# Gates interleaved with the first output row's product, and a first chunk loaded through ScalarE's queue, in a one-core RWKV-7 layer

## The chip, the cores and the metric

The kernel runs on one core of a Trainium2 chip. The metric is device time in microseconds (us), the median of several executions; less is better. The program is one launch that computes three blocks of a language model for one sequence of 1024 tokens of width 1024, in float32.

## The reference, cut to what matters

The model is a Hawk block (a gated linear recurrence), a feed-forward network (FFN) with a gated per-layer embedding (PLE), then an RWKV-7 block with its own FFN and PLE, and a block with a state-space branch and attention. The change is in the RWKV-7 block. Its core, per head of 64 channels, is a recurrence over the tokens:

```python
def step(S, inp):
    r_t, w_t, k_t, v_t, a_t, b_t = inp
    sa = jnp.einsum('bhvk,bhk->bhv', S, a_t)
    S = S * w_t[:, :, None, :] + sa[..., None] * b_t[:, :, None, :] + v_t[..., None] * k_t[:, :, None, :]
    y = jnp.einsum('bhvk,bhk->bhv', S, r_t)
    return S, y
...
yn = ((y - mean) * lax.rsqrt(var + RW_GN_EPS)).reshape(B, T, D)
yn = yn * ln_w.astype(f32) + ln_b.astype(f32)
...
g = jax.nn.sigmoid(xg @ g1) @ g2
out = (yn + bonus.reshape(B, T, D)).astype(x.dtype) * g
return out @ w_o, v_first
```

The output of the recurrence is normed per head, multiplied by a gate `g` (a product with the matrix g2, 160 rows), and multiplied by `w_o` (1024 by 1024); the result is added to the residual stream `h`.

## The kernel before, in words

**Layout and order.** The sequence is cut into two halves of 512 tokens. Activations stand as eight tiles of 128 channels by 512 tokens. The kernel is written as Python generators (FFN, PLE, recurrence, ...), and a helper `both` interleaves two of them by weights, so that TensorE has dense matmuls from the one beside the many small steps of the other. Every engine (TensorE, VectorE, ScalarE, GpSimd, SyncE) runs its own instruction list strictly in order. That order is fixed when the program is built: a planner goes through the program with costs of its own, and each engine takes of the instructions that are ready by the planner's reckoning the one that stands first in the program.

**Matmuls in float32.** Each product of a weight matrix with an activation is made of three faster ones, on a high part and a low part of each operand (`mm3`, L188 to L198: hi by hi at L196, hi by low at L197, low by hi at L198). A high part is a cast on ScalarE (L61 for weights, L201 for activations), a low part a subtraction on VectorE (L64 and L66 for weights, L202 for activations). With 8 blocks of 128 channels an output row of 128 channels by 512 tokens takes 24 matmuls.

**Weights.** `Weights` streams all matrices in one fixed order through two raw buffers, loaded on SyncE's queue (L52), and three pairs of split buffers. `get(key)` returns the next matrix and first makes sure that it and the one behind it have been split.

**The recurrence, `rw_b`.** It is called once per half, interleaved with FFN work. A half has 8 chunks of 64 tokens. `load(c)` loads a chunk's operands from DRAM, where earlier steps left them: the tile AR (L1030), KB in three loads (L1034 and twice L1038) and ST in two (L1043), all on SyncE's queue. `load_cp` loads for a pair of chunks the triangular tables TT (L1054) and T1 (L1055, T in the profile), twice each, and V (L1057). The first products of a half are those of AR with the state (L1138), then AR by KB (L1094), then those of T and TT (L1068). The tables are written to DRAM by the step before, in stores that SyncE issues as VectorE finishes them (L1009 for ttD, L1011 for t1D); the last of these stand right ahead of `load(0)` on SyncE's queue. The norm's weight `lnw` is one 4 KB piece a partition, the first tile of the recurrence's pool; it is loaded on GpSimd's queue (L1020) and read at the end of a pair of chunks (L1221). Tiles are placed in memory in the order in which they are allocated, and a new tile waits for the last use of the tiles whose memory it takes.

**The gate and the output, `rw_c`.** It is called once per half behind the recurrence. Eight gate steps come first: four matmuls with the two pieces of g2 (L1285), one VectorE operation that adds the bias to the normed output `qt` and multiplies it by the gate (L1286), and the split into high and low part. The `qt` tiles are loaded on GpSimd's queue, two at a time in half 1 and all four in half 0. Then come eight output rows m: the row's matrix ("ro", half, m), a load of `h`, `mm3` over the eight gated operands, the addition to `h` (L272), and the squares for the next norm. In half 0 six gate steps run alone, then a deferred norm of the other half, then the rest interleaved with `rw_shift(1)`, which is mostly VectorE work. In half 0 PSUM has the pools "mm" (3 banks), "g" (3) and two single ones; in half 1 "mm" (6) and "aux" (2).

Of the kernel before, what the change touches and what calls it, by code (L numbers as in the profile page):

```python
# [9 lines left out]
F32 = mybir.dt.float32  # L10
# [7 lines left out]
D = 1024  # L18
# [11 lines left out]
class Weights:  # L30
# [44 lines left out]
    def view(t, kp, nk, m):  # L75
        return t[0:kp, 0:nk * m].rearrange("p (k m) -> p k m", m=m)

    def get(self, key):
        i = self.pos
        assert self.jobs[i][0] == key, (self.jobs[i][0], key)  # L80
        n = len(self.jobs)
        while len(self.loaded) < min(n, i + self.nraw):
            if len(self.loaded) >= self.nraw + len(self.ready):
                self._split(len(self.ready))
            else:
                self._load(len(self.loaded))
        while len(self.ready) < min(n, i + 2):
            self._split(len(self.ready))
            if len(self.loaded) < n:
                self._load(len(self.loaded))  # L90
        self.pos += 1
        r = self.ready[i]
        self.ready[i] = None
        return r


class Kernel:
# [763 lines left out]
    def rw_elem(self, half, ap):  # L861
# [7 lines left out]
        def at(tag, bufs=2, dt=F32, n=HALF):  # L869
            return self.t512(tag, bufs, dt, n, ap)  # L870
# [25 lines left out]

        def products(j, AR, KB, rk):
            pb = self.psum("g")
# [7 lines left out]
            for ch in range(8):  # L906
                cp, par = ch // 2, ch % 2
                o = 64 if par == 0 else 0
                for e in range(2):
                    rows = slice(e * 64, e * 64 + 64)  # L910
                    nc.tensor.matmul(pe[e][o:o + 64, cp * 64:cp * 64 + 64], KB[rows, cp, 1 + par, :],
                                     AR[rows, cp, 1 + par, :], start=True, stop=True)
            for e in range(2):
# [11 lines left out]
        for j in range(8):  # L925
# [12 lines left out]
            s, c, kk = at("t_s", 1), at("t_c", 1), at("t_k", 1)  # L938
            AR = ap.tile([128, 4, 4, 64], F32, tag="AR", name="AR", bufs=2)
            KB = ap.tile([128, 4, 4, 64], F32, tag="KB", name="KB", bufs=2)  # L940
            R, K = AR[:, :, 0:4:3, :], KB[:, :, 0:4:3, :]
            A, B = AR[:, :, 1:3, :], KB[:, :, 1:3, :]
            B3 = B.rearrange("p a b c -> p a (b c)")
# [20 lines left out]
            gtt(out=R, in0=R, in1=v4(rr), op=MUL)  # L964
            nc.sync.dma_start(out=self.arD[half][j], in_=AR.rearrange("p a b c -> p (a b c)"))
            nc.sync.dma_start(out=self.kbD[half][j], in_=KB.rearrange("p a b c -> p (a b c)"))
# [47 lines left out]
    def rw_b(self, half, bp):  # L1014

        nc = self.nc
        tt = nc.vector.tensor_tensor
        mm = nc.tensor.matmul
        self.lnw = bp.tile([128, D], F32, name="lnw")
        nc.gpsimd.dma_start(out=self.lnw, in_=self.i["rw_ln_w"].to_broadcast([128, D]))  # L1020
        st = {}

        def odd(t, e, a=0, n=16):

            return t.rearrange("p (h v) -> p h v", v=64)[:, a + e:a + n:2, :]

        def load(c):
            s = st.setdefault(c, {})
            AR = bp.tile([128, 8, 128], F32, tag="AR", name="AR", bufs=2)
            nc.sync.dma_start(out=AR, in_=self.arD[half][:, :, c * 128:(c + 1) * 128].rearrange("j p x -> p j x"))  # L1030
            KB, src = bp.tile([128, 8, 128], F32, tag="KB", name="KB", bufs=2), self.kbD[half]

            r = self.hp(c % 2)
            nc.sync.dma_start(out=KB[r], in_=src[:, r, c * 128:(c + 1) * 128].rearrange("j p x -> p j x"))  # L1034
            r = self.hp(1 - c % 2)
            for a in range(2):
                o = c * 128 + (1 - a) * 64
                nc.sync.dma_start(out=KB[r, :, a * 64:(a + 1) * 64], in_=src[:, r, o:o + 64].rearrange("j p x -> p j x"))  # L1038
            s.update(AR=AR, KB=KB)

            s["ST"] = bp.tile([128, D], F32, tag="ST", name="ST", bufs=2)
            for e in range(2):
                nc.sync.dma_start(out=s["ST"][self.hp(e), :], in_=self.vD[half * 4 + c // 2, self.hp(c % 2), :])  # L1043

        def load_cp(cp):
            s = st.setdefault(("cp", cp), {})

            TT = bp.tile([128, 16, 64], F32, tag="TT", name="TT", bufs=2)
            T1 = bp.tile([128, 16, 32], F32, tag="T1", name="T1", bufs=1)
            for sd in range(2):  # L1050
                r = sd * 64
                of = lambda t: t.rearrange("x (h e a c) t -> x h e a (c t)", e=2, a=4, c=2)[:, :, 1 - sd, cp, :]
                to = lambda t: t.rearrange("x (h c) t -> x h (c t)", c=2)
                nc.sync.dma_start(out=to(TT[r:r + 64]), in_=of(self.ttD))  # L1054
                nc.sync.dma_start(out=to(T1[r:r + 32]), in_=of(self.t1D[half]))  # L1055
            V = bp.tile([128, D], F32, tag="V", name="V", bufs=2)
            nc.sync.dma_start(out=V, in_=self.vD[half * 4 + cp])  # L1057
            s.update(V=V, TT=TT, T1=T1)
# [42 lines left out]
        def kbt(c):  # L1101
# [3 lines left out]
            for g in range(2):  # L1105
# [3 lines left out]
                nc.scalar.copy(out=s["KT"][:, g * 512:(g + 1) * 512], in_=p)  # L1109

        load(0)
        load_cp(0)
        load(1)
        gram(0)
        merge(0)
# [3 lines left out]
        for c in range(8):  # L1119
# [5 lines left out]
            G, AR, KT, ST = s["G"], s["AR"], s["KT"], s["ST"]  # L1125
# [6 lines left out]
            for g in range(2):  # L1132

                for j in range(4 * g, 4 * g + 4):
                    for a in range(2):
                        for e in range(2):
                            r, o = self.hp(e), self.hp((a + e + c) % 2)
                            mm(zy[e][o, hs(j)], AR[r, j, a * 64:(a + 1) * 64], self.S[r, j, :], start=j == 0,  # L1138
                               stop=False, skip_group_check=True)
                for h in range(8 * g, 8 * g + 8):  # L1140
                    e = h % 2
                    mm(zy[e][ru[e], hs(h // 2)], G[rv[e], h, ga:ga + 64], ST[rv[e], hs(h)],
                       start=False, stop=False, skip_group_check=True)

                for e in range(2):
                    (nc.scalar.copy if e == 0 else nc.vector.tensor_copy)(
                        out=odd(Z, e, 8 * g, 8), in_=zy[e][:, g * 256:(g + 1) * 256].rearrange("p (h v) -> p h v", v=64))
            yield
            pp = self.psum2()
            for g in range(2):  # L1150
                p = pp[:, g, :]
# [3 lines left out]
                for e in range(2):  # L1155
                    (nc.scalar.copy if e == 0 else nc.vector.tensor_copy)(out=odd(ST[ru[e], :], e, 8 * g, 8),
                                                                          in_=odd(p[ru[e], :], e, 0, 8))
            pp = self.psum2()
            yield
            for g in range(2):  # L1160
                ps = pp[:, g, :]
                for h in range(8 * g, 8 * g + 8):
                    r = slice((h % 2) * 64, (h % 2) * 64 + 64)
# [16 lines left out]
            for g in range(2):  # L1180
                for h in range(8 * g, 8 * g + 8):
                    e = h % 2
                    mm(zy[e][rv[e], hs(h // 2)], G[:, h, gr:gr + 64], ST[:, hs(h)],
                       start=False, stop=True, skip_group_check=True)
                for e in range(2):
                    nc.scalar.copy(out=odd(Y[self.hp(c % 2), :], e, 8 * g, 8),
                                   in_=zy[e][rv[e], g * 256:(g + 1) * 256].rearrange("p (h v) -> p h v", v=64))
# [3 lines left out]
            if c < 6:  # L1191
                load(c + 2)
# [76 lines left out]
    def rw_c(self, half, op, nout, qs):  # L1269

        nc = self.nc
        tt = nc.vector.tensor_tensor
        hs = slice(half * HALF, (half + 1) * HALF)
        sh, sl, s3 = self.sg
        w = [self.W.get(("rg2", half, 0)), self.W.get(("rg2", half, 1))]
        o = {}
        for j in range(8):
            if j % 2 == 0 and len(self.qt) <= j // 2:
                next(qs)
            qt = self.qt[j // 2][:, j % 2, :]  # L1280
            p = self.psum()
            (wh, wl), (w3, _) = (tuple(t[:, 0, j * 128:(j + 1) * 128] for t in a) for a in w)
            pairs = ((wh, sh), (wh, sl), (wl, sh), (w3[0:96], s3[0:96, :]))
            for n, (a, x) in enumerate(pairs):
                nc.tensor.matmul(p, a, x, start=n == 0, stop=n == 3)  # L1285
            nc.vector.scalar_tensor_tensor(out=qt, in0=qt, scalar=self.v("rw_ln_b", j), in1=p, op0=ADD, op1=MUL)  # L1286
            hi, lo = (op.tile([128, HALF], F32R, tag=f"{q}{j}_{half}", name="o") for q in ("hi", "lo"))
            self.split(hi, lo, qt)
            o[j] = (hi, lo)
            yield  # L1290
        for m in range(8):
            wm = self.W.get(("ro", half, m))
            h = self.h[m, half]
            nc.sync.dma_start(out=h, in_=self.hD[m, :, hs])
            p = self.psum()
            self.mm3(p, wm, lambda k: o[k], 8)
            self.add_h(m, half, p)
            self.norm_sq(nout, m, half)
            if op is not nout["pool"][half]:
                self.norm_split(nout, m, half)  # L1300
            yield
        if op is nout["pool"][half]:
            for m in range(8):
                self.norm_split(nout, m, half)
        self.norm_done(nout, half)
# [910 lines left out]
```

## Time and profile before

| what | value |
|---|---|
| median of the runs | 3542.28 us (3541.84 to 3548.24, 3 runs) |
| the profiled execution | 3545.02 us |
| its span in the trace | 3543.3 us |
| TensorE busy | 3368.8 us, 95% of the span |
| VectorE busy | 2318.8 us, 65% |
| ScalarE busy | 1573.8 us, 44% |
| GpSimd busy | 720.2 us, 20% |
| mean granted TensorE clock | 0.97 of full speed |

The profile is of one execution. Its own time is 2.7 us above the median of the three runs; the span is what its trace covers. Busy time is that of the engine's instructions; DMA issues on a queue are not counted in it. In the rows below PE is TensorE, PEld its loading of weights, DVE VectorE, ACT ScalarE, POOL GpSimd, SP SyncE; ACTq and SPq are an engine's issuing of DMAs. A time in brackets is how long the engine stood idle before the instruction, and what ended the idle time.

### The profile page before, as it was taken

The numbers are of one execution on the slowest core, as the hardware profiler recorded it, in microseconds if no ns is written. First come the engines' busy times: TensorE is split into PE (matmuls) and PEld (weight loads), VectorE is DVE, ScalarE is ACT, GpSimd is POOL, SyncE is SP. The second block draws the span as 40 slices with busy tenths as digits, with TensorE's granted clock in tenths as the row PEclk, the third lists the DMA queues.
The fourth block names the chain that finished last, engine by engine and source line by source line (L and its number), as shares of the span: only waits on it lengthen the run. The fifth ranks groups of instructions, "written<-read, shape, count | busy, mean of one in ns | idle before, by whom it ended". The sixth has DMA issues, their size and how long they took to land. (4 is left out here: it accounts for less than half of the span.)

```text
span 3543.3 us, 51794 instructions
## 1 busy us (share of the span) xinstructions
PE 3368.8 (95%) x19883; PEld 2699.7 (76%) x19883; DVE 2318.8 (65%) x3793; ACT 1573.8 (44%) x2420; POOL 720.2 (20%) x1162
## 2 busy tenths in 40 slices
PE   7999899999999989999999899999999999998999
PEld 6777687787767767777677677777888888776777
DVE  7676867776657586576765875566444477676664
ACT  6656622233434552355455523434222254477453
POOL 4222448840300120011201200001000033230020
PEclk8999999999999998999999999999999999999999
DMA  3111113433534677545336756543232222330524
GB/s 102 41 50 46 38 43 105 127 119 92 162 101 122 180 191 152 130 118 163 116 114 175 202 140 146 125 122 114 84 110 87 68 74 82 102 101 24 184 87 116
DMA packets 645191, 394.76 MB, mean 111 GB/s; under 512 B 119492, under 2 KB 597488, under 8 KB 644944
## 3 DMA queue, kind: packets, MB, share of 16 engines
q1 hardware_dynamic: 637504, 377.28, 37.9%
q0 software_dynamic: 3488, 10.06, 0.9%
q10 hardware_dynamic: 3952, 4.13, 0.4%
q8 instruction: 156, 2.56, 0.3%
q14 instruction: 91, 0.75, 0.1%
HBM read 321.45 MB, written 69.93 MB: 110 GB/s over the span
## 5 line engine op out<-in xcount | busy, mean ns | idle before, releaser
L61 ACT CAST whi<-wr 128x1024 fp32r<-128x1024 f32 (+3 forms) x566 | 478.3, 848 | 1050.9 <-PE mm L197 634.3
L196 PE MATMUL mm<-hgh,whi 128*128 128x512 f32 x2272 | 909.4, 400 | 7.9 <-ACT whi L61 5.4
L198 PE MATMUL mm<-hgh,wlo 128*128 128x512 f32 x2272 | 900.0, 396 | 2.4 <-DVE wlo L66 1.8
L197 PE MATMUL mm<-hgl,whi 128*128 128x512 f32 x2272 | 900.0, 396 | 2.2 <-DVE hgl L229 2.2
L66 DVE TENSOR_TENSOR wlo<-wr,whi 128x1024 fp32r<-128x1024 f32 (+3 forms) x564 | 572.0, 1016 | 319.7 <-ACT whi L61 304.8
L196 PEld LDWEIGHTS mm<-hgh,whi 128*128 128x128 f32 x2272 | 433.6, 191 | 108.5 <-issue 9.9
L198 PEld LDWEIGHTS mm<-hgh,wlo 128*128 128x128 f32 x2272 | 432.9, 191 | 98.8 <-DVE wlo L66 5.5
L197 PEld LDWEIGHTS mm<-hgl,whi 128*128 128x128 f32 x2272 | 433.8, 191 | 95.5 <-issue 2.8
L575 DVE TENSOR_TENSOR f<-mm,rstd 128x512 f32<-128x512 f32 x176 | 120.7, 687 | 268.0 <-PE mm L198 267.8
L196 PE MATMUL mm<-mh,whi 128*128 128x512 f32 x704 | 277.6, 401 | 9.7 <-ACT mh L201 4.3
L198 PE MATMUL mm<-mh,wlo 128*128 128x512 f32 x704 | 276.2, 397 | 7.2 <-DVE wlo L66 6.6
L197 PE MATMUL mm<-ml,whi 128*128 128x512 f32 x704 | 279.0, 397 | 2.1 <-DVE ml L202 2.1
L243 POOL TENSOR_TENSOR acc<-acc,sq 128x512 f32<-128x512 f32 x84 | 131.1, 1561 | 709.1 <-PE mm L197 384.5
L272 DVE TENSOR_TENSOR h<-mm,h 128x512 f32<-128x512 f32 x272 | 182.1, 683 | 71.3 <-PE mm L198 70.8
L196 PEld LDWEIGHTS mm<-mh,whi 128*128 128x128 f32 x704 | 133.3, 190 | 44.8 <-issue 5.7
L198 PEld LDWEIGHTS mm<-mh,wlo 128*128 128x128 f32 x704 | 133.8, 190 | 41.0 <-DVE wlo L66 13.2
L197 PEld LDWEIGHTS mm<-ml,whi 128*128 128x128 f32 x704 | 133.7, 190 | 30.6 <-DVE ml L202 3.7
L197 PE MATMUL mm<-xl,whi 128*128 128x512 f32 (+2 forms) x320 | 126.6, 398 | 0.0
L198 PE MATMUL mm<-xh,wlo 128*128 128x512 f32 (+2 forms) x320 | 126.2, 396 | 0.4 <-DVE wlo L66 0.3
L196 PE MATMUL mm<-xh,whi 128*128 128x512 f32 (+2 forms) x320 | 122.8, 395 | 1.3 <-ACT kt L829 1.3
L201 ACT CAST mh<-f 128x512 fp32r<-128x512 f32 x88 | 54.7, 621 | 153.4 <-DVE f L580 153.4
L997 POOL MEMSET lnT<- 128x1024 f32 x4 | 3.8, 956 | 470.7 <-DVE w2l L891 382.2
(624 smaller groups left out, 6006.9 us busy)
## 6 DMA issues: line engine op xcount, KB each, us to landing
wr<-in_ffn_w_in_dram SPq DMA_DIRECT2D x162, 512.0 KB, 3.9
wr<-in_ffn_w_out_dram SPq DMA_DIRECT2D x120, 256.0 KB, 2.8
wr<-in_rw_w_rkv_dram SPq DMA_DIRECT2D x48, 512.0 KB, 4.2
wr<-in_ple_w_gate_dram SPq DMA_DIRECT2D x24, 512.0 KB, 4.2
wr<-in_ffn_w_out_dram SPq DMA_DIRECT2D x56, 192.0 KB, 2.5
wr<-in_lru_w_in_dram SPq DMA_DIRECT2D x20, 512.0 KB, 3.8
wr<-in_w_in_dram SPq DMA_DIRECT2D x18, 512.0 KB, 4.1
hD<-h SPq DMA_DIRECT2D x32, 256.0 KB, 2.0
```

What stands on the lines that cost most here:

```text
L61: self.nc.scalar.copy(out=hi[s], in_=t[s])
L66: self.nc.vector.tensor_tensor(out=lo[s], in0=t[s], in1=f32(hi[s]), op=SUB)
L196: mm(ps, a, xh, start=start and k == 0, stop=False)
L197: mm(ps, a, xl, start=False, stop=False)
L198: mm(ps, b, xh, start=False, stop=stop and k == nk - 1)
L201: self.nc.scalar.copy(out=hi, in_=src)
L243: nc.gpsimd.tensor_tensor(out=a, in0=a, in1=q, op=ADD)
L272: self.nc.vector.tensor_tensor(out=h, in0=ps, in1=h, op=ADD)
L575: tt(out=t, in0=p, in1=nin["rstd"][half], op=MUL)
L997: nc.gpsimd.memset(X, 0.0)
```

## The change

Three edits:

- In `rw_b`, the loads of AR and KB of chunk 0 (four DMAs per half) are issued from ScalarE's queue instead of SyncE's. ST of chunk 0, and the loads of all later chunks, stay on SyncE's.
- The tile `lnw` is allocated, and its load issued, after `load(0)` instead of before it. AR, KB and ST then lie 4 KB a partition lower, and `lnw` lies behind them.
- In `rw_c`, the matrix of output row 0 is fetched before the gates (a new argument `ahead` of `get` lets it be split without the one behind it), a PSUM tile of its own is taken for the row (from pool "g" in half 0, from "mm" in half 1), and its product is made in pieces of three matmuls: that of block k stands behind gate step k + 2, the last two where row 0's product stood. The matrices of rows 1 and 2 are both split at row 1.

```diff
--- before.py
+++ after.py
@@ -75,7 +75,7 @@
     def view(t, kp, nk, m):
         return t[0:kp, 0:nk * m].rearrange("p (k m) -> p k m", m=m)
 
-    def get(self, key):
+    def get(self, key, ahead=2):
         i = self.pos
         assert self.jobs[i][0] == key, (self.jobs[i][0], key)
         n = len(self.jobs)
@@ -84,7 +84,7 @@
                 self._split(len(self.ready))
             else:
                 self._load(len(self.loaded))
-        while len(self.ready) < min(n, i + 2):
+        while len(self.ready) < min(n, i + ahead):
             self._split(len(self.ready))
             if len(self.loaded) < n:
                 self._load(len(self.loaded))
@@ -1016,8 +1016,6 @@
         nc = self.nc
         tt = nc.vector.tensor_tensor
         mm = nc.tensor.matmul
-        self.lnw = bp.tile([128, D], F32, name="lnw")
-        nc.gpsimd.dma_start(out=self.lnw, in_=self.i["rw_ln_w"].to_broadcast([128, D]))
         st = {}
 
         def odd(t, e, a=0, n=16):
@@ -1026,16 +1024,18 @@
 
         def load(c):
             s = st.setdefault(c, {})
+
+            q = nc.scalar if c == 0 else nc.sync
             AR = bp.tile([128, 8, 128], F32, tag="AR", name="AR", bufs=2)
-            nc.sync.dma_start(out=AR, in_=self.arD[half][:, :, c * 128:(c + 1) * 128].rearrange("j p x -> p j x"))
+            q.dma_start(out=AR, in_=self.arD[half][:, :, c * 128:(c + 1) * 128].rearrange("j p x -> p j x"))
             KB, src = bp.tile([128, 8, 128], F32, tag="KB", name="KB", bufs=2), self.kbD[half]
 
             r = self.hp(c % 2)
-            nc.sync.dma_start(out=KB[r], in_=src[:, r, c * 128:(c + 1) * 128].rearrange("j p x -> p j x"))
+            q.dma_start(out=KB[r], in_=src[:, r, c * 128:(c + 1) * 128].rearrange("j p x -> p j x"))
             r = self.hp(1 - c % 2)
             for a in range(2):
                 o = c * 128 + (1 - a) * 64
-                nc.sync.dma_start(out=KB[r, :, a * 64:(a + 1) * 64], in_=src[:, r, o:o + 64].rearrange("j p x -> p j x"))
+                q.dma_start(out=KB[r, :, a * 64:(a + 1) * 64], in_=src[:, r, o:o + 64].rearrange("j p x -> p j x"))
             s.update(AR=AR, KB=KB)
 
             s["ST"] = bp.tile([128, D], F32, tag="ST", name="ST", bufs=2)
@@ -1109,6 +1109,8 @@
                 nc.scalar.copy(out=s["KT"][:, g * 512:(g + 1) * 512], in_=p)
 
         load(0)
+        self.lnw = bp.tile([128, D], F32, name="lnw")
+        nc.gpsimd.dma_start(out=self.lnw, in_=self.i["rw_ln_w"].to_broadcast([128, D]))
         load_cp(0)
         load(1)
         gram(0)
@@ -1274,6 +1276,13 @@
         sh, sl, s3 = self.sg
         w = [self.W.get(("rg2", half, 0)), self.W.get(("rg2", half, 1))]
         o = {}
+
+        w0 = self.W.get(("ro", half, 0), 1)
+        p0 = self.psum("g" if "g" in self.ps_bufs else "mm")
+
+        def first(k):
+            self.mm3(p0, w0, lambda _: o[k], 1, k, start=k == 0, stop=k == 7)
+
         for j in range(8):
             if j % 2 == 0 and len(self.qt) <= j // 2:
                 next(qs)
@@ -1287,13 +1296,20 @@
             hi, lo = (op.tile([128, HALF], F32R, tag=f"{q}{j}_{half}", name="o") for q in ("hi", "lo"))
             self.split(hi, lo, qt)
             o[j] = (hi, lo)
+            if j > 1:
+                first(j - 2)
             yield
         for m in range(8):
-            wm = self.W.get(("ro", half, m))
             h = self.h[m, half]
             nc.sync.dma_start(out=h, in_=self.hD[m, :, hs])
-            p = self.psum()
-            self.mm3(p, wm, lambda k: o[k], 8)
+            if m == 0:
+                for k in (6, 7):
+                    first(k)
+                p = p0
+            else:
+                wm = self.W.get(("ro", half, m))
+                p = self.psum()
+                self.mm3(p, wm, lambda k: o[k], 8)
             self.add_h(m, half, p)
             self.norm_sq(nout, m, half)
             if op is not nout["pool"][half]:
```

## Rows read from the trace of the kernel before

**Rows 1.** Page of the profile, part 1: busy time of each engine

```profile
PE 3368.8 (95%) x19883; PEld 2699.7 (76%) x19883; DVE 2318.8 (65%) x3793; ACT 1573.8 (44%) x2420; POOL 720.2 (20%) x1162
```

**Rows 2.** TensorE's waits: line, who was waited for: us in total, times, longest us

```profile
PE zy L1138 <- DMA AR<-arD: 8.4, 2, 5.1
...
PE gg L1094 <- DMA KB<-kbD: 2.6, 4, 1.0
...
PE mm L197 <- DVE o L202: 4.5, 1, 4.5
```

**Rows 3.** Timeline of TensorE: start us, us, engine, line, operation [idle before <- releaser]

```profile
1396.02 0.70 PE L1138 MATMUL zy<-S,AR 64*64 64x64 f32 x14 [5.12 <-DMA AR<-arD]
...
1405.05 1.14 PE L1068 MATMUL gg<-T,TT 32*32 32x32 f32 x61 [0.78 <-DMA T<-t1D]
...
2115.59 0.46 PE L1138 MATMUL zy<-S,AR 64*64 64x64 f32 x14 [3.30 <-DMA AR<-arD]
...
2123.95 1.27 PE L1068 MATMUL gg<-T,TT 32*32 32x32 f32 x40 [0.41 <-DMA T<-t1D]
...
2397.30 0.64 PE L1285 MATMUL mm<-sgh,whi 128*128 128x512 f32 x1 [3.89 <-DVE h L272]
```

**Rows 4.** Windows: length, busy PE, PEld, DVE, ACT, POOL, granted clock, DMA share, GB/s

```profile
1380.00:1390.00 10.00, 10.00 (x46) 8.29 (x45) 6.66 (x11) 3.36 (x4) 0.00 (x0) 1.00 0.86 181
...
1394.00:1404.00 10.00, 6.94 (x105) 6.45 (x106) 3.20 (x5) 0.00 (x0) 0.00 (x0) 0.50 1.15 203
...
1408.00:1421.00 13.00, 13.00 (x117) 10.35 (x116) 0.42 (x1) 2.31 (x5) 1.74 (x2) 0.50 1.03 202
...
2124.00:2141.00 17.00, 17.00 (x217) 13.74 (x218) 1.07 (x3) 4.21 (x8) 2.55 (x2) 0.50 1.17 228
...
1469.50:1475.00 5.50, 4.71 (x83) 3.97 (x83) 4.28 (x5) 4.48 (x7) 0.00 (x0) 0.50 0.32 62
```

**Rows 5.** Timeline of SyncE's queue at the start of half 0

```profile
1381.97 3.33 SPq L1009 DMA_DIRECT2D ttD<-lnN  x2
...
1387.08 0.84 SPq L1030 DMA_DIRECT2D AR<-arD  x1
1387.96 2.51 SPq L1034 DMA_DIRECT2D KB<-kbD  x1
1390.51 1.65 SPq L1038 DMA_DIRECT2D KB<-kbD  x2
1392.20 2.31 SPq L1043 DMA_DIRECT2D ST<-vD  x2
...
1397.28 0.57 SPq L1055 DMA_DIRECT2D T<-t1D  x1
```

**Rows 6.** Timeline of SyncE's queue at the start of half 1

```profile
2109.07 0.62 SPq L1030 DMA_DIRECT2D AR<-arD  x1
2109.73 1.09 SPq L1034 DMA_DIRECT2D KB<-kbD  x1
2110.86 2.07 SPq L1038 DMA_DIRECT2D KB<-kbD  x2
```

**Rows 7.** Timeline of ScalarE ahead of the start of half 0

```profile
1384.40 1.05 ACT L61 CAST whi<-wr 128x1024 fp32r<-128x1024 f32 x1 [1.19 <-PE mm L197]
```

**Rows 8.** Lines: issues on ScalarE's queue in this kernel (ns min/median/max)

```profile
L1254 ACTq DMA_DIRECT2D sg<-sgD x6: 309/441/1127, 1653.2 to 2371.4; - x6
```

**Rows 9.** DMA issues: count, KB each, median us to landing

```profile
AR<-arD SPq DMA_DIRECT2D x16, 512.0 KB, 6.4
```

**Rows 10.** Lines: the first readers of lnw (first and last start)

```profile
L1221 DVE TENSOR_TENSOR Y<-Y,lnw x8: 1214/1216/1216, 1472.6 to 2355.1; 128x1024 f32<-128x1024 f32 x8
```

**Rows 11.** Timeline of VectorE in the gates of half 1

```profile
2395.21 1.22 DVE L64 TENSOR_TENSOR whi<-wr,whi 32x1024 fp32r<-32x1024 f32 x1 [1.01 <-ACT whi L61]
...
2412.40 2.49 DVE L202 TENSOR_TENSOR o<-qt,o 128x512 fp32r<-128x512 f32 x4
```

**Rows 12.** Timeline of ScalarE in the gates of half 1

```profile
2406.14 2.00 ACT L61 CAST whi<-wr 128x1024 fp32r<-128x1024 f32 x2 [1.77 <-PE mm L1285]
```

## The prediction

> **What bounds the kernel now.** I read the page first: TensorE is busy 95% of the span [rows 1], so a change gains only where TensorE stands idle or runs at a lower clock. Then its waits, grouped by the matmul that waited [rows 2]. The change touches these groups. The state recurrence's first products wait for the AR tile, 8.4 us in two waits, and the products with KB wait another 2.6 us in four: the two starts of `rw_b`, one per half of the sequence. In `rw_c` a product of half 0 waits 4.5 us for the low part of a gated operand (L202); the first gate of half 1 waits 3.89 us for an addition on VectorE (L272), as the last of TensorE's rows shows [rows 3].
>
> The other rows of that group give the places of the starts. In half 0 its last dense matmul is over by 1390.9, and it then waits 5.12 us for AR (to 1396.02); in half 1 it waits 3.30 us (to 2115.59). Some 9 us later in each half it waits again, 0.78 and 0.41 us, for the triangular table T of line 1068. T is loaded last of what the first chunk needs: this second wait is short now because the first one covers it.
>
> The windows [rows 4] show what a start costs beyond its idle time. From 1394 to 1404 and from 1408 to 1421 the granted clock is 0.50, the lower level (1.2 of 2.4 GHz); in half 1 it is 0.50 from 2124 to 2141. TensorE is busy 13.00 of 13 us and 17.00 of 17 us there, so at full clock those two stretches alone would be shorter by 6.5 + 8.5 = 15 us. Such a stretch follows an idle one; a shorter one stands at 1469.5 to 1475.
>
> SyncE's issues in half 0 [rows 5]: two ttD stores, a weight load, AR at 1387.08, KB in three loads, ST at 1392.20, then the tables, the last T at 1397.28. AR is in use 8.9 us after its issue begins. Half 1 has the same order [rows 6].
>
> **AR and KB of chunk 0 on ScalarE's queue.** Four issues leave SyncE's queue and join ScalarE's. By program order they come behind ScalarE's work of that moment, the last of which before them is the cast at 1384.40 or the one before it [rows 7]; AR's issue would begin between 1382.6 and 1385.5 instead of 1387.08. ScalarE's own issues of this kind have a median of 0.44 us and at most 1.13 [rows 8], so four take 1.8 to 4.5 us of ScalarE; behind them stand casts of ffn weights that are split one matrix ahead, which is the cover; without it the casts' delay, up to 4.5 us once per half, would stand on TensorE. I take nothing. AR's median landing over 16 loads is 6.4 us [rows 9]: from 1383.2 that is 1389.6, before TensorE's arrival at 1390.9; with its present 8.9 us, 1392.1. So 1.2 us at most of the 5.12 stays; KB's waits go likewise.
>
> That is not the gain, since T is late next. SyncE's queue is rid of 0.84 + 2.51 + 1.65 us, 5.1 with the gaps: ST could be issued at 1387.08 instead of 1392.20 and the tables as much sooner. The tables read what the ttD stores wrote; those are issued by 1385.3, and if they take as long as AR's 6.4 us, the first table can go no sooner than 1391.7, 3.1 us earlier than now if it follows ST as it does today. In half 1 the four issues take 0.62 + 1.09 + 2.07 = 3.8 us. By issue, then, T comes 3.1 to 5.1 us sooner in half 0 and 3.8 in half 1.
>
> The transfers set another limit. From 1380 to 1390 the DMA engines are already busy 0.86, and 1.15 from 1394 to 1404 [rows 4]. Before TensorE runs dry there is room for (1.15 - 0.86) / 1.15 = 25% of the 7 us from 1383 to 1390: 1.8 us of transfer. The same bytes must land before T, so by this T comes 1.8 us sooner. The Trainium skill ("DMA: Bandwidth & Descriptors", section "Issuing engines are not separate DMA queues") speaks against the change in the same way: loads started by several engines run on the same 16 DMA engines and interleave, and starting them from two saves only issue time, usually small beside the transfer. By that rule alone the sum would be the 3.6 us of the first rival below; by the issues in the rows it would be 8 to 9. The traces bear both: issues of 2.51 us are not small, and 0.86 is not idle.
>
> I take 3 us in each half, between 1.8 and 5.1 (3.8): **6 us**, bounds 3.6 and 8.9.
>
> **The clock behind it.** TensorE would now do its AR and KB products from 1391, some 5 us of work at full clock, and idle before T for 4 to 6 us instead of before AR. An idle stretch of that kind has been followed by half clock everywhere in these rows, so I don't expect the whole 15 us. If the stretch that follows were as short as that at 1469.5 (5.5 us), the rest would be worth (13 - 5.5)/2 + (17 - 5.5)/2 = 9.5 us; if it lasts as long as today, nothing. The present ones are in just this code, so I lean to the lower side: **5.5 us**, bounds 0 and 15.
>
> **lnw behind the chunk's tiles.** Its load is issued a few steps later on GpSimd's queue and its first reader is at 1472.6 [rows 10], some 80 us after the new place: nothing, and some 80 us of cover. AR, KB and ST move down by lnw's 4 KB a partition, onto memory whose earlier tiles were used up long before; nothing again, since no load there waits today for a reader of old memory. If a tile there were still in use, the first load would wait and the first rival would hold.
>
> **`rw_c`.** No instruction is added: the product of output row 0 (24 matmuls) is moved among the gates, with a PSUM bank of its own, and the split of ro0 is asked for before the gates without that of ro1. TensorE has the same work, so only idle time can change.
> In half 1 gate 0 took the bank that L272 still read; the bank now goes to the product, and the gate takes a free one. Gate 0 still needs the 32-row piece that VectorE splits from 2395.21 to 2396.43 [rows 11], for its fourth matmul; that was at about 2398.5, three steps of some 0.4 us behind 2397.30: a gain of 2.1 us. Against it: ro1's split (a cast of 1.0 us, half of the row of two that waits for the last gate at 2406.14 [rows 12], then 1.2 us on VectorE as in the row at 2395.21) was hidden under row 0's product, which now lies in front of it: a loss of up to 2.2 us. The two cancel. In half 0 the wait of 4.5 us is for VectorE, which has the same list of work in another order; by that row it can go either way by 4.5 us. I take nothing for all of `rw_c`, bounds -6.6 and +6.7.
>
> **The rivals.**
> First, T lands hardly sooner, since the DMA engines are the limit. For it: the busy share of 0.86 ahead of the start. Against it: 2.51 and 1.65 us of mere issue on SyncE. This is also where the rule of the Trainium skill quoted above leads. Gain 2 x 1.8 = 3.6 us and the half clock as it is: 3542.3 - 3.6 = 3539, no change that can be told. Chance 0.24.
> Second, T lands as soon as its issue allows, and the clock stays high in both starts: 8.9 + 15 = 24 us, 3518. [...] Against it: T needs its 6 to 8 us after ttD has landed, so TensorE idles anyway. Chance 0.16.
> Third, the other side: the product of row 0 stands in TensorE's fixed order ahead of work that could run. In half 1 the last four gated operands are finished by VectorE only from 2412.40 to 2414.89 [rows 11]. Today the products of rows 0, 1 and 2 with the first four operands, 36 matmuls, fill the time from the last gate at 2406.1 [rows 12] to nearly the end of that (0.23 us each). If row 0's twelve are spent among the gates, which then end 2.8 us later, and its last twelve (2.8 us) stand before row 1's, TensorE idles from 2408.9 to 2414.9 but for these 2.8 us: 3.2 us, and half clock behind it costs some 2.7 (half of a 5.5 us stretch). In half 0 the same with the 4.5 us wait doubled. Together 10.4; with the first rival's gain of 3.6, +6.8; with both stretches of clock (2.7 more) +9.5: 3552. It decides where the load part gives less than 3.4 us beside it. For it: both waits stand in the rows, and the order is fixed beforehand. Against it: today's order does place other rows' matmuls before the late operands. Chance 0.14.
>
> **How the numbers follow.** The profiled execution took 3545.0 us (span 3543.3), 2.7 over the median of the runs, 3542.3. Sum: 6 + 5.5 + 0 = 11.5 us; 3545.0 - 11.5 = 3533.5 as profiled, 3530.8 against the median: **3531**. Its own chance is 0.46 (gain 7.1 to 17). 0.2% is 7.1 us, about what a measurement can tell from no change. Faster 0.46 + 0.16 = 0.62, same 0.24, slower 0.14. The likeliest case and the first rival span 3525 to 3542; the range goes out to most of the second (3515) and to the near half of the third (3547), which leaves out about 0.15. Forecast case by itself: 3525 to 3535.
>
> **What would show it.** Right: in the rows of line 1138 the waits for AR are under 1.5 us in each half; the second batch of line 1068 starts about 1402 and 2121 (from 1405.05 and 2123.95) behind a wait for T of 3 us and more; the granted clock is back at 1.00 sooner than 1421 and 2141; AR's load stands on ScalarE's queue before 1386; gate 0 of half 1 no longer waits for L272. Wrong: AR lands as late as before, or T does; the half-clock stretches keep their length; TensorE's waits for line 202 or for a weight split grow in `rw_c` by more than the starts give.

## The result: slower by 0.8%

The changed kernel takes 3575.99 us (median of 4 runs, 3567.67 to 3578.6) beside 3542.8 us for the kernel before on the same chip: a ratio of 1.0083, 95% interval 1.0064 to 1.0102, so some 29 us are lost (the two medians lie 33 us apart). Forecast was 3531 us and a range up to 3547: wrong in direction. Of the experiments below, one execution (of the loads alone, 4426.22 us) lay far above the others of its kernel, and the ratio of that run is formed without it.

### The profile page after: what moved, and what is told of

It is laid out like the page before. It is cut to its first block, busy times and chain, and to the rows that moved or that the text cites. A ratio compares the mean times of both kernels' runs of the same rounds, so it can differ in the third digit from the quotient of the medians.

```text
span 3572.0 us, 51796 instructions
## 1 busy us (share of the span) xinstructions
PE 3371.7 (94%) x19883; PEld 2701.1 (76%) x19883; DVE 2319.9 (65%) x3793; ACT 1572.9 (44%) x2420; POOL 721.5 (20%) x1162
## 5 line engine op out<-in xcount | busy, mean ns | idle before, releaser
L66 DVE TENSOR_TENSOR wlo<-wr,whi 128x1024 fp32r<-128x1024 f32 (+3 forms) x564 | 571.8, 1015 | 330.4 <-ACT whi L61 315.5
L272 DVE TENSOR_TENSOR h<-mm,h 128x512 f32<-128x512 f32 x271 | 181.2, 682 | 85.5 <-PE mm L198 84.7
```

Of the source, the lines that this page charges most:

```text
L66: self.nc.vector.tensor_tensor(out=lo[s], in0=t[s], in1=f32(hi[s]), op=SUB)
L272: self.nc.vector.tensor_tensor(out=h, in0=ps, in1=h, op=ADD)
```

## The profile after

The new file has other line numbers: line 1138 is now 1140, 1230 is 1232, 1285 is 1294. TensorE's waits of the changed kernel, whole span:

```profile
PE mm L198 <- DVE wlo L66: 22.4, 17, 7.8
PE gg L1094 <- DMA KB<-kbD: 17.2, 2, 9.3
...
PE gg L1232 <- DVE Y L1226: 9.7, 1, 9.7
...
PE mm L1294 <- DVE h L272: 4.2, 1, 4.2
```

The wait for AR [rows 2] is gone, as forecast. The one for KB has grown from 2.6 us to 17.2, in two waits. A wait of 9.7 us for Y (the recurrence's output for a pair of chunks, which VectorE norms) at line 1232 is new: before, nothing waited for Y there. The wait for a weight's low part (L66) was 14.7 us and at most 1.8 before. The four places, in TensorE's timeline:

```profile
1407.19 1.13 PE L1094 MATMUL gg<-AR,KB 64*64 64x128 f32 x16 [9.34 <-DMA KB<-kbD]
...
1705.19 0.79 PE L198 MATMUL mm<-o,wlo 128*128 128x512 f32 x1 [7.79 <-DVE wlo L66]
...
2132.46 0.92 PE L1094 MATMUL gg<-AR,KB 64*64 64x128 f32 x12 [7.89 <-DMA KB<-kbD]
...
2388.69 1.09 PE L1232 MATMUL gg<-ident,Y 128*128 128x128 f32 x4 [9.74 <-DVE Y L1226]
```

Why KB is late stands in ScalarE's timeline at the start of half 0:

```profile
1386.23 0.63 ACT L577 ACTIVATE f<-f 128x512 f32<-128x512 f32 x1 [1.54 <-DVE f L575]
1386.24 0.39 ACTq L1030 DMA_DIRECT2D AR<-arD  x1
1386.67 1.05 ACTq L1034 DMA_DIRECT2D KB<-kbD  x1
1393.67 5.08 ACTq L1038 DMA_DIRECT2D KB<-kbD  x2
1398.79 0.62 ACT L201 CAST mh<-f 128x512 fp32r<-128x512 f32 x1 [11.92 <-DMA KB<-kbD]
```

AR and the first KB load go out at once. The second KB load begins 6 us later, and the cast behind the loads is held for 11.92 us. The row of two covers the second and the third; by the view of KB's tile they begin at 1393.7 and 1398.2 (ns of the issue, first and last start):

```profile
L1038 ACTq DMA_DIRECT2D KB<-kbD x2: 581/584/586, 1393.7 to 1398.2; - x2
```

SyncE's queue in the same stretch:

```profile
1385.63 5.10 SPq L1009 DMA_DIRECT2D ttD<-lnN  x2
1390.83 2.29 SPq L52 DMA_DIRECT2D wr<-in_ffn_w_in_dram  x1
1393.17 1.23 SPq L1043 DMA_DIRECT2D ST<-vD  x2
...
1399.35 0.57 SPq L1055 DMA_DIRECT2D T<-t1D  x1
```

And how long the first of the two ttD stores, and the weight load, took from issue to landing (views by line, of that stretch):

```profile
L1009 SPq DMA_DIRECT2D ttD<-lnN x2: 1054/2526/3997, 1385.6 to 1386.7; - x2
...
DMA to landing us min/median/max: 8.0/8.0/8.0
```

```profile
L52 SPq DMA_DIRECT2D wr<-in_ffn_w_in_dram x1: 2293/2293/2293, 1390.8 to 1390.8; - x1
...
DMA to landing us min/median/max: 7.3/7.3/7.3
```

1385.63 + 8.0 = 1393.6 and 1390.83 + 7.3 = 1398.1: the moments at which the two KB loads are issued. In the program, the DMAs of SyncE's and ScalarE's queues take eight completion flags (semaphores that count a DMA's landing) in turn, and each waits until the DMA that had its flag before it, the eighth before it, has landed. For the second and third KB load of chunk 0 these are that store and that load: the instruction records of the trace name the same flag for the store and the second KB load (semaphore 100), and for the weight load and the third (103), and both KB loads wait for it. On one queue such a pair stands far apart; on two queues the KB loads stand level with what they wait for. Half 1 is alike (issues at 2120.46 and 2125.4).

Windows of the changed kernel (columns as in [rows 4]), the second from TensorE's last state product of half 1 to line 1232:

```profile
2199.00:2212.00 13.00, 12.48 (x85) 9.53 (x86) 5.90 (x8) 3.72 (x8) 1.90 (x1) 0.50 0.58 137
...
2377.20:2388.60 11.40, 1.75 (x12) 1.07 (x8) 10.25 (x14) 4.51 (x7) 0.00 (x0) 0.77 0.06 17
```

VectorE and ScalarE norm the last pair of chunks in the second window, and TensorE has 12 matmuls in it, 6 of them dense FFN matmuls. Before, 68 dense ones stood there, and TensorE was busy throughout:

```profile
2348.30:2363.80 15.50, 15.50 (x74) 12.79 (x71) 13.20 (x17) 8.93 (x12) 0.00 (x0) 1.00 0.21 61
```

Such dense matmuls, which keep TensorE busy while other engines work, are called cover below. In the middle of half 1 the clock is at 0.50 for 13 us; before, it was 1.00 from 2160 to 2260.

## The experiments

Theory A: the loads moved to ScalarE are the cause. Theory B: the product moved in `rw_c` is. Four runs took the change apart. Ratios are to the kernel before on the same chip.

**The loads alone** (line `q = nc.scalar if c == 0 else nc.sync` and the three lines that use it for four loads).

> Of the three edits only the first: AR and the three KB loads of chunk 0 are issued on ScalarE's queue; lnw and rw_c are as before. Theory A (the loads moved are the cause: the last two KB loads are issued only when earlier transfers have landed, and TensorE's order in half 1 is worse): most of the loss, 15 to 33 us slower than before, TensorE waits 7 us or more for KB in each half. Theory B (the cause is the product moved among the gates): within 5 us of before, KB waits under 2 us.

Measured: ratio 1.0057 (1.0040 to 1.0074), some 20 us. KB waits 17.9 us in two, and Y 9.7.

**The product in `rw_c` alone.**

> Of the three edits only the last: the product of output row 0 among the gates. Theory A: -3 to +6 us against before (the trace of the changed kernel shows 4 us lost in the gates of half 0 and nothing in those of half 1). Theory B: 15 to 30 us slower, with the loss in the gates.

Measured: ratio 1.0048 (1.0033 to 1.0063), some 17 us (14 by the medians), which neither theory had: TensorE waits 9.5 us for Y in the recurrence of half 1, of which this kernel changes no line.

**lnw alone.**

> Of the three edits only the second: lnw is allocated and loaded after the first chunk's loads. Both theories: within 4 us of before. If it is slower by more, the place of AR and KB in memory matters, which neither theory has.

Measured: 0.9991 (0.9979 to 1.0004): nothing.

**AR alone on ScalarE's queue** (KB's three loads stay on `nc.sync`).

> Only AR of chunk 0 goes through ScalarE's queue; KB stays on SyncE's, rw_c and lnw as before. Theory A: the KB loads are again issued in a row on SyncE's queue, so the wait of 8 to 9 us for KB is gone; -8 to +4 us against before. Rival (any load on ScalarE's queue at this place costs, by delayed casts or by another order of TensorE): 10 us slower or more, as with all four.

Measured: 1.0010 (0.9996 to 1.0025), and a wait of 7.6 us for Y. A load on ScalarE's queue isn't dear by itself.

So both edits cost, and both have the wait for Y. 20 + 17 less one such wait of 9.6 is 27, near the 29 of both together; but each of the three has an interval of 5 to 7 us either way, so the sum by itself settles nothing. Theory C: an edit anywhere ahead makes the planner give the recurrence of half 1 another order, in which the FFN matmuls are used up early. Two runs put the edit of `rw_c` into one half:

```diff
+        new = half == 0        # the other run: half == 1
+        if new:
+            w0 = self.W.get(("ro", half, 0), 1)
...
-            if j > 1:
+            if new and j > 1:
...
-            if m == 0:
+            if new and m == 0:
```

> Only the product among the gates, and only in half 0. Theory C: 8 to 17 us slower, and most of it in the recurrence of half 1, 600 us later, of which no line differs: a wait of 9 us for Y, with 7 dense matmuls between the last state product and line 1230 in place of 68. Rival: the loss is in the gates of half 0, none in the recurrence of half 1.

Measured: ratio 1.0039 (1.0027 to 1.0050), 14 us. Window and wait of half 1 in this run:

```profile
2356.80:2368.10 11.30, 1.89 (x11) 1.24 (x7) 10.18 (x14) 4.51 (x7) 0.00 (x0) 0.77 0.06 17
```

```profile
PE gg L1232 <- DVE Y L1226: 9.5, 1, 9.5
```

> Only the product among the gates, and only in half 1; its gates come after both recurrences, so the order of the recurrences is that of before. Theory C (what the edits cost outside the KB wait is the order that the planner then gives the recurrence of half 1: FFN matmuls are used up early and none are left to cover the last norm): within 4 us of before, TensorE's wait for Y at line 1230 under 1 us. Rival (the moved product costs by itself, as in the third rival of the prediction): 5 to 10 us slower, the loss in the gates of half 1.

Measured: ratio 1.0000 (0.9989 to 1.0011). The same window:

```profile
2342.10:2357.60 15.50, 15.50 (x74) 12.79 (x71) 13.21 (x17) 8.93 (x12) 0.00 (x0) 1.00 0.21 61
```

Theory C holds: the edit in half 1, behind both recurrences, is free; the one in half 0 costs 14 us, and 9.5 of it stand 600 us later in a part that no edit touches. From the last t1D store ahead of half 1's recurrence to the first gate behind it, the run with the edit in half 0 takes 304.4 us; three executions with the order of before (the kernel before, lnw alone, the edit in half 1) take 290.3 to 294.9. TensorE is busy all of the window with 74 matmuls, or idle for most of it with 11.

Then the cover was given back by hand, with FFN steps that used to follow the loop:

```diff
-                    go(both((self.rw_b(1, bp), 44), (islice(f, 36), 36)))
+                    go(both((self.rw_b(1, bp), 44), (islice(f, 40), 36)))
...
-                for _ in range(4):
+                for _ in range(0):
                     next(f)
```

> The whole change, and four more FFN steps of half 1 go into the recurrence's loop (40 for 36; before, they followed it at once), behind its last step in program order. By the program 60 dense matmuls then stand between the last state product and line 1230 in place of 6. Theory C: the wait of 9.7 us for Y falls under 1 us and the whole is 8 to 14 us faster than the changed kernel, so 15 to 21 us slower than before; the KB waits stay at 8 to 9 us. Rival (cover is not the cause, the time goes to clock and waits wherever the order puts them): as the changed kernel, 29 us slower than before.

Measured: ratio 1.0054 (1.0035 to 1.0072), 10 us better than the change as it was. In half 1 the wait for Y is gone, that for KB stays, and one for the cast of the next weights appears behind the loop, where the four steps had been the cover:

```profile
PE gg L1094 <- DMA KB<-kbD: 8.1, 1, 8.1
PE mm L196 <- ACT whi L61: 5.0, 3, 4.6
```

> AR alone on ScalarE's queue, with the same four FFN steps moved into the loop: 69 dense matmuls in place of 15 as the cover. Theory C: its wait of 7.6 us for Y goes too, 4 to 10 us faster than before. Rival: as AR alone, 0 to 7 us slower than before.

Measured: 1.0000 (0.9987 to 1.0012): the wait for Y goes, one of 5.2 us for the cast comes. The rival's number, by theory C's mechanism less a price that it had left out.

Theory D is that of the completion flags. The last two KB loads go to GpSimd's queue, which has flags of its own:

```diff
-                q.dma_start(out=KB[r, :, a * 64:(a + 1) * 64], in_=src[:, r, o:o + 64].rearrange("j p x -> p j x"))
+                (nc.gpsimd if c == 0 else q).dma_start(out=KB[r, :, a * 64:(a + 1) * 64], in_=src[:, r, o:o + 64].rearrange("j p x -> p j x"))
```

> The whole change, but the last two KB loads of chunk 0 are issued on GpSimd's queue; AR and the first KB load stay on ScalarE's. By the program the loads on ScalarE's and SyncE's queues share eight completion flags in turn, so that each is issued only when the eighth before it has landed; GpSimd's have flags of their own. Theory D (the KB wait is this: the last two KB loads stand behind the landings of a ttD store and of a weight load): TensorE's wait for KB falls from 9.3 and 7.9 us to under 3 us in each half, and ScalarE is no longer held for 12 us. Rival (KB lands late because the DMA engines are full): the KB wait stays at 6 us or more. The cover of the norm is 20 matmuls in place of 6 here, so a wait for Y of 5 to 8 us stays; in all 8 to 22 us slower than before by D, 20 to 29 by the rival.

Measured: ratio 1.0014 (1.0005 to 1.0023), 5 us, where the change had 29: less than the 8 that theory D gave at least. No wait for KB is left in either half. ScalarE's timeline:

```profile
1385.42 0.39 ACTq L1030 DMA_DIRECT2D AR<-arD  x1
1385.85 1.41 ACTq L1034 DMA_DIRECT2D KB<-kbD  x1
1387.36 1.05 ACT L61 CAST whi<-wr 128x1024 fp32r<-128x1024 f32 x1 [1.31 <-PE mm L198]
1388.32 0.62 ACT L201 CAST mh<-f 128x512 fp32r<-128x512 f32 x1
```

The casts follow at once. The DMA engines are about as full as in the changed kernel (share 1.03 from 1384 to 1394 and 1.01 in the next 10 us, beside 1.01 and 1.12), so the KB wait was not theirs. The order differs as well, so the 24 us are not the flags' alone. What is left in half 1 is a wait for the tables and one for Y:

```profile
PE gg L1232 <- DVE Y L1226: 7.4, 1, 7.4
PE gg L1068 <- DMA T<-t1D: 6.3, 2, 4.7
```

Three more runs tried the cover with two FFN steps in place of four (`islice(f, 38)`, and two in the loop behind).

> The loads as in the run with KB's last two on GpSimd's queue, but lnw and rw_c as before, and two more FFN steps of half 1 in the recurrence's loop (38 for 36), which gives 68 dense matmuls of cover as before the change. Theories C and D together: no long wait for KB or Y is left, 2 to 12 us faster than before. Rival (the waits at the two starts only move on to the tables, at the same cost): within 3 us of before.

Measured: 1.0037 (1.0024 to 1.0050), 13 us slower: a miss.

> AR alone on ScalarE's queue, and 38 FFN steps in the loop: 63 dense matmuls of cover, and two steps left behind the recurrence to cover the split of the first weights of the gates (with 40 TensorE waited 5.2 us there). Theory C: 2 to 10 us faster than before. Rival: within 3 us of before, as with 40.

Measured: 1.0004 (0.9995 to 1.0012): the rival's.

> Control: the kernel before with 38 FFN steps in the loop and nothing else (83 dense matmuls of cover for 68). It has no wait for Y to lose: within 3 us of before by every theory.

Measured: 1.0021 (1.0012 to 1.0029): a miss too. The steps moved cost 7 us by themselves; TensorE waits 5.1 us for a cast of weights behind the loop in all three. The other 6 us of the first are not settled: from the last t1D store ahead of half 0's recurrence to the first gate behind it, its profiled execution takes 283.7 us and that of the whole change with KB on GpSimd's queue 274.8 (three with the order of before: 278.6 to 285.5), and its order has waits of 2 to 4 us there (for the copy mX, for ST) that the other has not.

The last run takes both causes away and leaves the FFN steps alone: the whole change with KB's last two loads on GpSimd's queue, and the product among the gates in half 1 only.

> The loads as in the run of the whole change with KB's last two on GpSimd's queue, lnw moved too, and the product among the gates in half 1 alone. By the program the cover of the last norm of half 1 is 68 dense matmuls again, as in the kernel before. Theories C and D together (KB's wait is that for completion flags, the rest is the order in which cover is spent): no wait for Y over 1 us, no wait for KB over 3 us, none of the 4 us lost in the gates of half 0: 4 to 14 us faster than before. Rival (the two starts give nothing, since the wait for the tables takes the place of that for AR): within 4 us of before.

Measured: 3530.76 us beside 3545.03, ratio 0.9962 (0.9948 to 0.9976), **13 us faster than before** (8 to 18) and faster than every other version. TensorE at the two starts, windows behind them, and two of SyncE's waits at the first:

```profile
1394.16 0.40 PE L1140 MATMUL zy<-S,AR 64*64 64x64 f32 x11
...
1402.64 0.28 PE L1068 MATMUL gg<-T,TT 32*32 32x32 f32 x2 [6.04 <-DMA T<-t1D]
1404.50 0.71 PE L1068 MATMUL gg<-T,TT 32*32 32x32 f32 x19 [1.58 <-DMA T<-t1D]
...
2110.77 0.28 PE L1068 MATMUL gg<-T,TT 32*32 32x32 f32 x2 [5.49 <-DMA T<-t1D]
2112.54 1.67 PE L1068 MATMUL gg<-T,TT 32*32 32x32 f32 x55 [1.49 <-DMA T<-t1D]
```

```profile
1400.00:1409.00 9.00, 4.78 (x86) 4.23 (x87) 2.16 (x4) 1.53 (x3) 1.60 (x1) 0.50 0.88 182
1410.00:1430.00 20.00, 17.86 (x240) 14.21 (x240) 6.55 (x11) 5.92 (x13) 2.48 (x1) 1.00 0.75 162
...
2120.00:2140.00 20.00, 20.00 (x326) 16.13 (x325) 10.47 (x17) 7.49 (x15) 2.14 (x1) 1.00 0.96 191
1394.00:1639.00 245.00, 227.93 (x3184) 184.36 (x3183) 147.34 (x225) 108.09 (x193) 24.37 (x15) 0.95 0.53 128
2103.00:2347.00 244.00, 233.67 (x3237) 187.28 (x3234) 138.99 (x209) 97.87 (x168) 7.84 (x4) 0.98 0.54 129
```

```profile
SPq L1055 <- DMA wr<-in_ffn_w_in_dram: 1.7, 1, 1.7
...
SPq L1054 <- DMA ttD<-lnN: 0.4, 1, 0.4
```

There is no wait for AR, KB or Y, and half 1 has its 68 dense matmuls ahead of line 1232 again. The whole start's idle time is one wait for T of 7 to 8 us per half, and the half clock lies over that wait: it is back at 1.00 by 1410 and 2120, where it was 0.50 until 1421 and 2141 before [rows 4]. TensorE's waits at the two starts are no shorter than before: 14.6 us for T, where AR, KB and T took 8.4 + 2.6 + 1.2 = 12.2; so the gain is not in these waits.

This gain is not that of the loads in any order. The run with the same loads, lnw and `rw_c` as before, and 38 FFN steps was 13 us slower than before, so the two lie 26 us apart, of which the steps moved account for 7. In the profiles 10 of the rest stand in the recurrence of half 0 (283.7 us from the t1D store to the gates beside 273.4), where the two differ in order from the first product with AR on. The loads with lnw and `rw_c` as before and 36 steps were not run.

## Why the prediction was wrong

**AR, right; KB, the first step that failed.** "KB's waits go likewise" took four loads on ScalarE's queue for four issues in a row. AR went out at 1386.24, in an execution that was by then 3.8 us behind the one before; less that, it is the early end of the range given, and TensorE did not wait for it. KB's last two stood behind the landings of a ttD store and of a weight load, and TensorE waited 17.2 us for KB where nothing was to be left. "I take nothing" for ScalarE was wrong for the same reason: it was held 11.9 us, for which 4.5 had been the bound. The trace before could have shown it: T's last issue at 1397.28 [rows 5] begins as the first KB load lands, 1387.96 plus the 9.3 us that are the longest of its line (1034). The bound of the transfers (the DMA engines' busy share) was not what set KB's wait.

**T, mis-sized in another way.** 3 us in each half were forecast for T. Where KB is not in the way (the last run), the second batch of line 1068 starts at 1404.50 beside 1405.05 before, with TensorE idle for T in front of it as forecast. Counted from the t1D store that wrote its table (1382.38 and 1380.86 in the two executions) that is 22.1 us beside 24.2, in half 1 20.3 beside 21.6; with two more executions whose recurrences have the order of before it is 21.9 to 24.6 and 21.5 to 22.2. T comes some 1.4 us sooner, nearer to the first rival (1.8) than to the forecast. Two things stand behind it. The ttD stores take 8.0 us to land in half 0 (4.8 before), and the tables wait for them; that the loads issued beside them are the reason, as in the first rival, is argued. And the last T load waits 1.7 us for a weight load that had its flag before: it goes out at 1396.95, beside 1397.28 before, although five us of issues have left its queue. That part is in no rival. The rule of the Trainium skill ("DMA: Bandwidth & Descriptors", section "Issuing engines are not separate DMA queues"), by which loads started from several engines share the same DMA engines and only issue time is saved, agrees with the small size.

**The clock, mis-sized.** What the first rival left out is that AR's and KB's products, done while T is awaited, no longer stand behind it, and that the half-clock stretch then lies over the wait. The mean granted clock over the recurrences, from the first product to line 1232, is 0.93 of 254 us and 0.95 of 248 before, and 0.95 of 245 and 0.98 of 244 in the best version (last two rows of its windows):

```profile
1396.00:1650.00 254.00, 239.40 (x3192) 193.01 (x3192) 146.39 (x225) 107.33 (x192) 23.80 (x15) 0.93 0.51 123
2116.00:2364.00 248.00, 244.20 (x3234) 196.19 (x3232) 138.90 (x208) 97.03 (x167) 7.60 (x4) 0.95 0.53 126
```

Time at half speed is 2 x (1 - mean) of each: 36 + 25 us before, 24 + 10 in the best version, and 27 us less at half speed would be worth 13.5, about its whole gain. But that is one execution of each. In two others whose recurrences have the order of before, the same sum is 30 + 15 us (lnw alone) and 20 + 15 (the edit in half 1), so by the recurrences' clock the gain lies between nothing and 13.5. Firmer is the mean granted clock of all executions beside each other: 0.9720 in 11 of the kernel before, 0.9748 in 6 of the best version, over spans of 3542.5 and 3528.9 us. At most 99 us are lost to the clock in the one and 89 in the other: some 10 of the 13 us, where 5.5 was taken and 15 was the bound. The starts are where most of it can lie: from 6 us ahead of the first product with AR to 50 us behind it, in both halves together, TensorE is busy at half clock for 13 us in the best version, and for 26, 36 and 44 in the three executions with the order of before. In the changed kernel half 1 has 0.93 of 265 us, 37 us at half speed, with idle times in new places.

**`rw_c`, half right.** In half 1 the edit is worth nothing, as forecast, but not by two terms that cancel: gate 0 still waits 4.2 us for L272, so the bank brought nothing. In half 0 it costs 3 to 4 us (by the starts of the same matmuls ahead of and behind the gates, in three runs), of the 4.5 given as a bound: the wait for L202 gives way to one of 7.8 us for a weight's low part, of the two matrices that are now both split at row 1.

**The order, a step that was missing.** The sum held the rest of the kernel still. It did not stay still: the recurrence of half 1 got another order from edits ahead of it, TensorE waits 9.7 us for Y, and more of it runs at half clock. The run with the edit in half 0 alone shows 14 us from this and the gates of half 0 together. That the planner's reckoning of time, shifted by the edits, is what changes the order is argued from how it works; the runs show that the order changes and what it costs.

The third rival had the sign, by a mechanism (matmuls of row 0 ahead of others in the gates) that the runs bear out for 4 us in half 0 alone.

## What to carry to other kernels

Before a DMA is moved to another engine's queue, look at what its issue waits for, not only how long the issue takes: where completion flags are shared in turn, a load on a second queue waits for a slow store or weight load on the first, and holds the whole compute engine that issues it. In a kernel whose order is planned as a whole, an edit's price is read from all of the trace: compare where the filler work stands in every stage, also those that the edit doesn't touch, and above all whether the last wait of a stage still has cover. An edit that frees the first operands can pay even when the next table is hardly sooner, if the work that it lets run was paid at half clock behind the wait; here it paid in one order of the program, and the same loads in another order lost.

## What was not expected of the hardware

The profiled executions of the kernel before and of the changed one have the same matmuls in the same order up to the first start, and were 3.8 us apart at 1375 us; those of the kernel before and of the edit in half 1 alone were 5.9 us apart there. That is 0.1 to 0.2% of the whole, so a gain of a few microseconds is not to be read from two profiles. The first of the two ttD stores took 8.0 us to land in the changed kernel; the same store took 4.8 before.
